# Layer 0's residual, first 1024 columns: transposed by VectorE in 32x32 blocks and placed by transfers, not by TensorE

## The chip, the cores and the metric

One core of one Trainium2 chip runs the whole program; the other cores are idle. The metric is device microseconds of one execution, as a median over runs. Engines are named as the profile names them: PE is TensorE's matmul side and PEld its weight loads, DVE is VectorE, ACT is ScalarE, POOL is GpSimd, and SP is the engine whose queue issues nearly all transfers. A transfer is issued by an engine's queue (SPq is SP's) and then moved by 16 DMA engines that all transfers share.

## The reference

A decoder trunk of two layers over 256 tokens of width 2048, all in float32. Layer 0 mixes the tokens with a gated MLP and a cross-attention, layer 1 with a latent attention (MLA) and a cross-attention; both end with a gated feed-forward block (width 5632) with a short causal convolution. Around the change this is what is computed (RMS norms written as `rmsnorm`):

```python
x = x + conv_ffn(rmsnorm(x, g_ffn[0]), w_ffn_up[0], conv_w[0], conv_b[0], w_ffn_down[0])   # end of layer 0
kv = rmsnorm(x, g_kv) @ w_kv_a            # start of layer 1: 2048 -> 512 + 64
c_kv = rmsnorm(kv[..., :512], g_kv_lat)
z = rmsnorm(x, g_mix[1]) @ w_in_b[0]
```

The products are made nearly float32-exact: each operand is split into a rounded high part and the rest (a low part), and three products (high by high, high by low, low by high) are added.

## The kernel before

**Layouts.** Outside the last part of the feed-forward block the residual stands feature-major, in the tile `xT` (`k.x`, 128 partitions by 16 blocks by 256 tokens): a partition is a feature, and a block is 128 features. Its two parts stand in `xhl` (two tiles of 8 blocks, each block 256 high and 256 low values), which is what every product reads. The feed-forward's down projection works the other way, token-major, on the tile `xt` (128 partitions by 2 token halves by 2048 features), so the residual is turned once before it (`Tokens.turn`, L1361 to L1368) and once after it, which is where the change lies.

**Turning to tokens (unchanged).** `turn(r)` lets DVE transpose 32x32 blocks of `xT` into a scratch tile `xs` (L1364), and four transfers on SP's queue place those blocks in `xt`, in pieces of 32 values, that is 128 bytes (L1368). It is done in four steps between the products of the up projection, for each of the two layers.

**The down projection.** Its rows come in three parts (`FF_GROUPS`), and each part has two phases `ph` of 1024 output columns. The stage of interest is the second phase of the last part in layer 0. It runs over six pairs of weight rows, n = 0 to 5. For each pair two weight tiles of 512 KB are loaded by SP's queue (L814, four buffers `raw` and two `gate`), split by ACT (high part, L709) and DVE (low part, L710), and used by 24 matmuls of 512 columns (L795, L796, L797). When a phase ends, DVE adds the sums to `xt` (`added`, L1407) and ACT takes squares for the next norm (L1430). Some of the first phase's work goes by a cheaper scheme whose sums go through `staged`, a tile in `xT`'s place, and are added to `xt` by `combine` (L1391 to L1398).

**Turning back.** The first phase of the last part completes columns 0 to 1023 of `xt`, the second phase columns 1024 to 2047. So the first half is turned back during the second phase: `Inner.begin` (L1422) hangs `turned(0)`, `turned(2)`, `turned(4)` and `turned(6)` behind the pairs n = 1 to 4 of that phase, each for two blocks. `turned` (L1432) lets PE transpose the four 128x128 squares of two blocks into one bank (`token_transpose`, L401, the matmuls are on L406), and `put` writes the high part (ACT, L1441), the low part (DVE, L1442) and the value itself into `xT` (ACT, L1443). The second half is turned in the same way behind the first products of layer 1 (`done`, L1447, `k.pending`); that isn't changed.

**What follows.** `layer_b` (L1079) begins with the product with `w_kv_a`: eight chunks of two blocks each, in the order of the blocks. Each chunk's weights (512 KB) are loaded by SP's queue (L108), split with a gain by ACT (L123) and DVE (L124) and used by 24 matmuls of 256 columns (L157, L158, L160). Chunk 0 needs blocks 0 and 1 of `xhl`, chunk 1 blocks 2 and 3, and so on.

**Order.** Each engine works through its own list in order. The lists are made before the run by a planner, which walks the program with a simulated clock and takes on each engine the instruction that stands earliest in the program among those it holds ready. The splits of the down projection are kept in their order by hand (`behind`, L700), and DVE's transposes and `combine` are kept in program order (`keep_in_program_order`). A transfer waits in SP's queue for its data and its buffer, and what stands behind it waits too.

Of the kernel before, what the change touches and what calls it, by code (L numbers as in the profile page):

```python
# [8 lines left out]
F32 = mybir.dt.float32  # L9
# [3 lines left out]
AF = mybir.ActivationFunctionType  # L13
ALU = mybir.AluOpType
AX = mybir.AxisListType

P = 128
D = 2048
S = 256
NB = D // P  # L20
# [1319 lines left out]
class Tokens:  # L1340
# [37 lines left out]
    def begin(self, ph, last):  # L1378
        self.ph, self.last = ph, last
        if ph == 0:  # L1380
            self.staged = self.k.ap.tile([P, 2, 4, 512], F32, tag="xT", name=self.k.uid("staged"))
        return {}
# [38 lines left out]
class Inner(Tokens):  # L1421
    def begin(self, ph, last):  # L1422
        super().begin(ph, last)
        return {"hooks": {n: [lambda n=n: self.turned(2 * n - 2)] for n in range(1, 5)}} if last and ph else {}

    def evict(self, tb, half, acc):
        j, o = self.added(tb, half, acc)
# [3 lines left out]

    def turned(self, k0):  # L1432
        k, nc = self.k, self.nc
        if k0 == 0:
            k.new_hl()
            k.x = k.ap.tile([P, NB, S], F32, tag="xT", name=k.uid("xT"))

        def put(b, acc):
            a = acc.rearrange("p (k s) -> p k s", k=2)
            hl = k.hl_tiles[b // 8][:, b % 8 : b % 8 + 2, :]  # L1440
            nc.scalar.activation(hl[:, :, :S], a, AF.Copy)  # L1441
            nc.vector.tensor_tensor(hl[:, :, S:], a, hl[:, :, :S].bitcast(F32), ALU.subtract)  # L1442
            nc.scalar.activation(k.x[:, b : b + 2, :], a, AF.Copy)  # L1443

        k.token_transpose(self.xt, k0, k0 + 2, put)
# [111 lines left out]
```

## Time and profile before

| | us |
|---|---|
| median of 3 runs | 2030.46 |
| lowest and highest run | 2029.62, 2032.41 |
| span of the profiled execution (first to last instruction) | 2027.8 |
| PE busy in that span | 2017.2 |
| DVE, ACT, POOL busy | 1618.2, 1167.1, 112.8 |

The profile gives for its execution the span alone, not a time of its own as the runs have it; the runs lie 1.8 to 4.6 us above the span, which is what lies around the first and the last instruction. Times inside the span are counted from its start. A matmul's row shows how long it was under way, and matmuls overlap, so a row's mean is not what it adds to the path; the chain of waits shows that, with the start of each piece and what it added.

### The profile page before, as it was taken

How to read it: one execution, taken by the hardware profiler on the slowest of the kernel's cores; microseconds unless marked ns; L12 is line 12 of the kernel's file. 1: busy time of each engine (PE TensorE's matmuls, PEld its weight loads, DVE VectorE, ACT ScalarE, POOL GpSimd, SP SyncE). 2: the span in 40 equal slices, each digit the busy share in tenths (PEclk: the TensorE clock that was granted, in tenths of full speed). 3: DMA queues.
4: the chain of work that ended last, by engine and by line, in shares of the span. 5: the costliest groups of instructions: out<-in, count | busy, mean ns of one | idle time of the engine just before them, and what ended most of it. 6: DMA issues, size and time to landing. Idle time of an engine off the chain costs nothing.

```text
span 2027.8 us, 38053 instructions
## 1 busy us (share of the span) xinstructions
PE 2017.2 (99%) x15136; PEld 1912.3 (94%) x15136; DVE 1618.2 (80%) x2433; ACT 1167.1 (58%) x1675; POOL 112.8 (6%) x169
## 2 busy tenths in 40 slices
PE   9999999999999999999999999999999999999998
PEld 8989999999889999899989999999988999889996
DVE  6866766778898788987878786777889878898787
ACT  6754744545565555655566675455566555565565
POOL 0000013100000000000002141400000000000000
PEclk9999999999999999999999999999999999999999
DMA  8876556688657676577656634568865767657764
GB/s 255 234 216 181 166 193 195 192 209 259 208 177 218 198 240 199 179 216 246 187 179 187 183 113 162 190 196 210 257 205 181 219 192 246 196 177 219 241 206 145
DMA packets 248263, 409.24 MB, mean 202 GB/s; under 512 B 71502, under 2 KB 78996, under 8 KB 248084
## 3 DMA queue, kind: packets, MB, share of 16 engines
q1 hardware_dynamic: 247892, 406.27, 65.4%
q8 instruction: 118, 1.93, 0.4%
q14 instruction: 61, 0.50, 0.1%
q10 hardware_dynamic: 192, 0.54, 0.1%
HBM read 400.46 MB, written 2.10 MB: 199 GB/s over the span
## 4 chain that ended last, share of the span: by engine, by line
PE 99%; DVE 0%; ACT 0%; issue 0%; ACTq 0%
PE ps L157 22%; PE ps L158 22%; PE ps L160 22%; PE ps L796 7%; PE ps L797 7%; PE ps L795 7%; PE ps L189 2%; PE ps L190 2%; PE ps L191 2%; PE ps L524 1%; PE ps L406 0%; PE ps L604 0%; PE ps L602 0%; PE ps L603 0%; PE ps L1236 0%; PE ps L1024 0%
## 5 line engine op out<-in xcount | busy, mean ns | idle before, releaser
L118 ACT ACTIVATE whi<-raw 128x1024 fp32r<-128x1024 f32 x484 | 512.7, 1061 | 513.1 <-PE ps L158 373.6
L119 DVE TENSOR_TENSOR wlo<-raw,whi 128x1024 fp32r<-128x1024 f32 x484 | 599.0, 1241 | 246.6 <-ACT whi L118 244.1
L157 PE MATMUL ps<-xhl,whi 128*128 128x256 f32 x3264 | 763.1, 277 | 0.0
L158 PE MATMUL ps<-xhl,whi 128*128 128x256 f32 x3264 | 761.5, 276 | 0.0
L158 PEld LDWEIGHTS ps<-xhl,whi 128*128 128x128 f32 x3264 | 612.8, 188 | 0.5
L157 PEld LDWEIGHTS ps<-xhl,whi 128*128 128x128 f32 x3264 | 612.7, 188 | 0.6
L160 PE MATMUL ps<-xhl,wlo 128*128 128x256 f32 x3264 | 436.6, 276 | 0.0
L160 PEld LDWEIGHTS ps<-xhl,wlo 128*128 128x128 f32 x3264 | 400.5, 188 | 0.0
L710 DVE TENSOR_TENSOR wlo<-raw,whi 128x1024 fp32r<-128x1024 f32 x112 | 134.3, 1220 | 31.5 <-ACT whi L709 30.3
L796 PE MATMUL ps<-wlo,h 128*128 128x512 f32 x404 | 157.3, 390 | 0.0
L797 PE MATMUL ps<-whi,h 128*128 128x512 f32 x404 | 157.2, 389 | 0.0
L709 ACT ACTIVATE whi<-raw 128x1024 fp32r<-128x1024 f32 x112 | 115.7, 1055 | 53.1 <-PE ps L158 37.3
L795 PE MATMUL ps<-whi,h 128*128 128x512 f32 x404 | 128.8, 390 | 0.0
L157 PE MATMUL ps<-mainhl,whi 128*128 128x256 f32 x512 | 119.7, 277 | 0.0
L158 PE MATMUL ps<-mainhl,whi 128*128 128x256 f32 x512 | 119.3, 276 | 0.0
L890 ACT ACTIVATE c<-a,cT 128x256 f32<-128x256 f32 x176 | 99.7, 592 | 32.2 <-DVE a L237 30.2
L709 ACT ACTIVATE whi<-xs 128x1024 fp32r<-128x1024 f32 x52 | 53.8, 1059 | 87.3 <-DVE xs L757 73.1
L158 PEld LDWEIGHTS ps<-mainhl,whi 128*128 128x128 f32 x512 | 96.0, 188 | 0.0
L157 PEld LDWEIGHTS ps<-mainhl,whi 128*128 128x128 f32 x512 | 95.9, 188 | 0.0
L795 PEld LDWEIGHTS ps<-whi,h 128*128 128x128 f32 x404 | 75.8, 188 | 15.7
L797 PEld LDWEIGHTS ps<-whi,h 128*128 128x128 f32 x404 | 75.8, 188 | 15.7
L796 PEld LDWEIGHTS ps<-wlo,h 128*128 128x128 f32 x404 | 75.9, 188 | 15.4
(378 smaller groups left out, 2896.6 us busy)
## 6 DMA issues: line engine op xcount, KB each, us to landing
raw<-in_w_ffn_up SPq DMA_DIRECT2D x352, 512.0 KB, 4.4
raw<-in_w_ffn_down SPq DMA_DIRECT2D x126, 512.0 KB, 4.5
raw<-in_w_out SPq DMA_DIRECT2D x64, 512.0 KB, 3.9
raw<-in_w_in_a SPq DMA_DIRECT2D x56, 512.0 KB, 4.2
gate<-in_w_ffn_down SPq DMA_DIRECT2D x38, 512.0 KB, 4.6
raw<-in_w_mem_kv SPq DMA_DIRECT2D x31, 512.0 KB, 4.8
sums<-in_w_ffn_down SPq DMA_DIRECT2D x48, 256.0 KB, 7.1
raw<-in_w_in_b SPq DMA_DIRECT2D x16, 512.0 KB, 4.1
```

The source lines that it names most:

```text
L118: nc.scalar.activation(hi[:, :n], raw[:, :n], AF.Copy)
L119: nc.vector.tensor_tensor(lo[:, :n], raw[:, :n], hi[:, :n].bitcast(F32), ALU.subtract)
L157: mm(acc[:, :S], wh, x[:, :S], start=first, stop=False)
L158: mm(acc[:, :S], wh, x[:, S:], start=False, stop=False)
L160: mm(acc[:, :S], wl, x[:, :S], start=False, stop=last)
L189: mm(acc, xh, wh, start=first, stop=False)
L709: self.behind(self.nc.scalar.activation(hi, w, AF.Copy))
L710: self.behind(self.nc.vector.tensor_tensor(lo, w, hi.bitcast(F32), ALU.subtract))
L795: mm(o, xh, wh, start=start, stop=False)
L796: mm(o, xh, wl, start=False, stop=False)
L797: mm(o, xl, wh, start=False, stop=stop)
L890: nc.scalar.activation(c, a, AF.Identity, scale=w(2), bias=w(3))
```

## The change

Columns 0 to 1023 of `xt` are no longer transposed by PE. After n = 1 and n = 2 of the last phase, `blocks(0)` and `blocks(1)` each take 512 columns (four blocks): DVE transposes 32x32 blocks into a scratch tile `xs`, once for each half of the tokens, and 16 transfers on SP's queue place them in `xT`, each 32 partitions by 8 pieces of 128 bytes. After n = 4 and n = 5, `operand` reads `xT` and writes the two parts of two blocks with one ACT and one DVE instruction; it is called for blocks 0 and 2 after n = 4, and for blocks 4 and 6 after n = 5. The tiles for `xhl` and `xT` are now taken in `blocks(0)`. Columns 1024 to 2047 are turned as before.

```diff
 class Inner(Tokens):
     def begin(self, ph, last):
         super().begin(ph, last)
-        return {"hooks": {n: [lambda n=n: self.turned(2 * n - 2)] for n in range(1, 5)}} if last and ph else {}
+        if not (last and ph):
+            return {}
+        hooks = {1 + h: [lambda h=h: self.blocks(h)] for h in range(2)}
+        hooks.update({n: [lambda b=b: self.operand(b) for b in range(4 * (n - 4), 4 * (n - 3), 2)] for n in (4, 5)})
+        return {"hooks": hooks}
+
+    def blocks(self, h):
+        k, nc = self.k, self.nc
+        if h == 0:
+            k.new_hl()
+            k.x = k.ap.tile([P, NB, S], F32, tag="xT", name=k.uid("xT"))
+        xs = k.tmp(self.pool, [P, 1024], "xs", 2)
+        s = xs.rearrange("p (r k a j) -> p r k a j", r=4, k=4, a=2)
+        for a in range(2):
+            src = self.xt[:, a, 512 * h : 512 * (h + 1)].rearrange("p (k r j) -> p r k j", r=4, j=32)
+            k.tc.keep_in_program_order(nc.vector.transpose(out=s[:, :, :, a], in_=src))
+        for r in range(4):
+            o = k.x[32 * r : 32 * (r + 1), 4 * h : 4 * (h + 1)].rearrange("i k (a q j) -> i q (k a) j", a=2, j=32)
+            for q in range(4):
+                nc.sync.dma_start(out=o[:, q], in_=s[32 * q : 32 * (q + 1), r].rearrange("i k a j -> i (k a) j"))
+
+    def operand(self, b):
+        k, nc = self.k, self.nc
+        x, hl = k.x[:, b : b + 2, :], k.hl_tiles[b // 8][:, b % 8 : b % 8 + 2, :]
+        nc.scalar.activation(hl[:, :, :S], x, AF.Copy)
+        nc.vector.tensor_tensor(hl[:, :, S:], x, hl[:, :, :S].bitcast(F32), ALU.subtract)
...
     def turned(self, k0):
         k, nc = self.k, self.nc
-        if k0 == 0:
-            k.new_hl()
-            k.x = k.ap.tile([P, NB, S], F32, tag="xT", name=k.uid("xT"))
```

## Rows read from the trace of the kernel before

**Rows 1.** The page: busy time by engine, and the clock granted to PE by slice.

```profile
PE 2017.2 (99%) x15136; PEld 1912.3 (94%) x15136; DVE 1618.2 (80%) x2433; ACT 1167.1 (58%) x1675; POOL 112.8 (6%) x169
...
PEclk9999999999999999999999999999999999999999
```

**Rows 2.** The page's chain that ended last, its shares by engine.

```profile
PE 99%; DVE 0%; ACT 0%; issue 0%; ACTq 0%
```

**Rows 3.** Busy time by 10 us stretch: each engine, clock, DMA share, GB/s.

```profile
1040.00:1050.00 10.00, 10.00 (x51) 8.30 (x50) 6.66 (x8) 7.16 (x14) 0.00 (x0) 1.00 0.66 205
1050.00:1060.00 10.00, 10.00 (x48) 8.24 (x47) 7.26 (x10) 6.14 (x12) 0.00 (x0) 1.00 0.24 79
```

**Rows 4.** The chain in order of time: start us, us added, piece.

```profile
1037.72 0.11 PE ps L406
...
1041.51 0.33 PE ps L406 x3
...
1043.70 0.44 PE ps L406 x4
...
1049.61 0.44 PE ps L406 x4
...
1055.54 0.43 PE ps L406 x4
...
1061.44 0.12 PE ps L157
...
1066.90 0.87 PE ps L406 x8
```

**Rows 5.** The transposes on L406 by source line: ns shortest/median/longest.

```profile
L406 PE MATMUL ps<-ident,xt x16: 270/272/273, 1037.6 to 1055.7; 128*128 128x128 f32 x16
```

**Rows 6.** Groups from 1037 to 1062: busy us, mean ns.

```profile
L1442 DVE TENSOR_TENSOR xhl<-ps,xhl 128x512 fp32r<-128x512 f32 x4 | 2.7, 685 | 1.1 <-ACT xhl L1441 1.1
...
L1443 ACT ACTIVATE xT<-ps 128x512 f32<-128x512 f32 x4 | 2.4, 594 | 3.2 <-DVE xhl L1442 3.2
L1441 ACT ACTIVATE xhl<-ps 128x512 fp32r<-128x512 f32 x4 | 2.3, 579 | 0.0
```

**Rows 7.** DVE in order of time: start us, us.

```profile
1038.32 1.22 DVE L1391 TENSOR_TENSOR xt<-xt,staged 128x1024 f32<-128x1024 f32 x1
...
1040.59 1.28 DVE L1407 TENSOR_TENSOR xt<-ps,xt 128x512 f32<-128x512 f32 x2
1041.79 1.21 DVE L710 TENSOR_TENSOR wlo<-raw,whi 128x1024 fp32r<-128x1024 f32 x1
```

**Rows 8.** DVE's block transposes on L1364 (1024 columns each), by source line.

```profile
L1364 DVE STREAM_TRANSPOSE xs<-xT x8: 1235/1240/1245, 412.5 to 1388.6; 128x1024 f32<-128x1024 f32 x8
...
  DMA xt<-xs: 1.5, 2
```

**Rows 9.** SP's issues by source line, ns: weights, then two kinds of 128-byte pieces.

```profile
L108 SPq DMA_DIRECT2D raw<-in_w_kv_a x8: 367/368/379, 1040.7 to 1065.0; - x8
...
L399 SPq DMA_DIRECT2D xraw<-in_x x32: 560/625/1169, 26.7 to 61.6; - x32
...
DMA to landing us min/median/max: 3.7/3.9/5.3
...
L1368 SPq DMA_DIRECT2D xt<-xs x32: 591/667/3811, 413.9 to 1398.8; - x32
```

**Rows 10.** SP in order of time, loads of w_kv_a: start us, us.

```profile
1043.03 0.38 SPq L108 DMA_DIRECT2D raw<-in_w_kv_a  x1
...
1046.32 1.50 SPq L108 DMA_DIRECT2D raw<-in_w_kv_a  x2
...
1057.15 0.37 SPq L108 DMA_DIRECT2D raw<-in_w_kv_a  x1
```

**Rows 11.** ACT in order of time: splits for n = 5 and for w_kv_a's chunks.

```profile
1048.96 2.01 ACT L709 ACTIVATE whi<-gate 128x1024 fp32r<-128x1024 f32 x2 [0.30 <-PE ps L797]
...
1054.95 2.56 ACT L123 ACTIVATE whi<-raw,gT 128x512 fp32r<-128x512 f32 x4 [1.30 <-PE ps L797]
```

## Prediction, as it was made before the result

> **What bounds the kernel now.** I read the page first, then the chain, then the stretch of the change. PE is busy for 2017.2 of 2027.8 us at the full clock in every slice [rows 1], which is the higher of its two levels (2.4 GHz), and 99% of the chain that ended last is PE [rows 2]. In the stretch of the change, 1037 to 1062 us, PE is busy without a gap, DVE for 6.7 to 7.3 us in ten and ACT for 6.1 to 7.2 [rows 3]. So nothing that ACT, DVE or SP save is worth any time here, and what they add costs none until it makes PE wait. The change can win only what its matmuls take on PE's path, and lose by making PE's operands late.
>
> **What is removed from PE.** Sixteen transposes, 0.27 us each under way [rows 5]. What they add to the path is in the chain: one for 0.11, three for 0.33, and three groups of four for 0.44, 0.44 and 0.43 [rows 4], together 1.75 us, or 0.11 each. The sixteen of the second half, unchanged, show the same price (0.87 for eight, [rows 4]). Gain: 1.75 us.
>
> A page of the Trainium skill speaks of another price: TensorE: Matmul & The Clock Gate, Part 4 (PE-mode transpose), gives about 275 ns for a transpose of 128x128 inside one kernel. By it the sum would be 16 x 0.275 = 4.4 us. The duration agrees with this trace (272), but the chain's step doesn't, as the transposes overlap.
>
> **What goes from ACT and DVE.** ACT loses the four copies into xT (4 x 0.594 us), keeps four high parts and DVE four low parts (579 and 685 ns, [rows 6]), now read from xT instead of PSUM. Worth nothing: neither engine is on the chain. DVE gains four block transposes of 512 columns. One of 1024 takes 1.24 us [rows 8], so about 0.65 each, 2.6 us in all. They need the finished columns, which are there after the last sum on L1407 at 1041.8 us (the last step of combine ends at 1039.5, [rows 7]). Ahead of the split that begins at 1041.79 they push it to 1045.5 at worst. That split is for n = 3, whose matmuls begin where the transposes of 1043.70 end (1044.14, [rows 4]); the second of its two weight tiles is wanted by about 1044.6, so it costs between 0 and 0.9 us. I take 0, because the first of the four can run before 1040.6 and a planner that puts the split first costs nothing.
>
> **What is added to SP and the transfers.** 32 issues, 16 for each half, each of 256 pieces of 128 bytes. No row has this size. Below is the weight load, also 256 pieces but long ones: 0.37 us each; above are the transfers with 128-byte pieces, 512 of them in 0.56 to 0.63 and 1024 in 0.59 to 0.67 [rows 9]. Between these I take 0.5 from start to start (nearest by count is the lower, by form the upper; ends 0.43 and 0.65 with the gap between issues). For landing I take 3.9 us, the median of the 64-KB transfers in 128-byte pieces [rows 9]. The movers have room: they are 24 to 66% busy between 1040 and 1060 [rows 3].
> - First half: its two transposes are done by about 1042.4. Sixteen issues at 0.5 make 8.0, with the three loads of w_kv_a that stand in this time [rows 10], 0.4 each, 9.2: the last is issued by 1051.6 and lands by 1055.5.
> - Second half: its issues follow, 8.0 more, last at 1059.6, landed by 1063.5. At 0.43 the landings are at 1054.4 and 1061.3, at 0.65 at 1057.9 and 1068.3.
>
> Behind the 32 in SP's queue stands the fifth load of w_kv_a (1057.15, [rows 10]). It would go at 1059.6, at worst 1064.4. It feeds chunk 4. The first chunk begins at 1061.44 on the chain and the transposes behind the second at 1066.90 [rows 4], so a chunk takes 2.73 us; behind chunks 1 and 2 come eight transposes each (0.87), so chunk 4 begins at 1074.1, or 1072.4 without the 1.75. A load issued at 1064.4 has some 4 us to land and, behind that, two splits on ACT of 0.64 (four take 2.56, [rows 11]) and a low part on DVE that I count at 0.7: it is there by 1070.4, 2 us early at worst. Cost 0.
>
> **What becomes a new wait.** `operand` waits on ACT for transfers, where the high part used to wait for PE. Blocks 0 and 1 are wanted by chunk 0 at 1061.4 less 1.75 = 1059.7. They are ready at 1055.5 + 0.58 + 0.69 = 1056.8 (1059.2 at the slow end): covered. Blocks 4 and 5 are wanted by chunk 2, behind the transposes of 1066.90, at 1066.90 + 0.87 - 1.75 = 1066.0. They are ready at 1063.5 + 1.27 = 1064.8: covered by 1.2 us, but not at the slow end (1069.6, 3.6 late). Queued behind a waiting `operand` on ACT are the splits of n = 5 (two at 1048.96) and of w_kv_a's chunks (four from 1054.95, [rows 11]), on DVE their low parts, and PE waits for all of these. This is the cover that the whole sum hangs on.
>
> **Sum.** -1.75 for PE, 0 for the rest: the span goes from 2027.8 to 2026.1. The page gives no time of its own for that execution; with the runs' median, 2.66 us above the span, the change gives 2030.46 - 1.75 = **2028.7 us**, 0.09% less. A measurement of this kernel tells about 0.2%, 4.1 us, from no change, so this counts as the same.
>
> **Rivals.**
> - *A late second half (B).* SP's issues go at 0.65 us, blocks 4 to 7 come 3.6 us late and PE waits once, at chunk 2: -1.75 + 3.6 = +1.9, 2032.3 us; from 2029.5 to 2034.5 over its bounds. For: the rows for 128-byte pieces all lie at 0.56 and above, and one of the issues took 3.8 us [rows 9]. Against: a quarter to a half of the pieces per issue. Still the same within 0.2%.
> - *ACT's list in the wrong order (C), slower.* If the planner believes the transfers to land earlier than they do, it places `operand` ahead of splits that PE needs sooner. ACT then stands at blocks 4 and 5 until 1068.3 with chunk 1's split behind it: two `operand` steps, two splits and a low part make it 1068.3 + 1.2 + 1.3 + 0.7 = 1071.5 where PE wants it at 1062.4 (1059.7 + 2.73): 9.1 - 1.75 = +7.4, 2038 us. The same with the first half, ahead of n = 5's splits, gives 6 us of stall, as these are wanted at 1055.97 - 1.75 = 1054.2 and the first comes at 1057.9 + 1.2 + 1.1 = 1060.2; that stall would be part of the other, not added to it. It decides against the change from a stall of 5.8 us (4.1 + 1.75). For: the planner's clock was behind the transfers where it last handled 128-byte pieces between engines (DVE waited 1.5 us on two transfers into xt, [rows 8]). Against: that was only 1.5 us in two places, and n = 5's splits end at 1051.0, 5 us ahead of PE [rows 11].
> - *The transposes cost more than their steps (D), faster.* If each took its 272 ns from the path [rows 5], the gain would be 4.35 us and the time 2026.1, 0.21% less. Against it stands the chain: four take 0.44 us and the next matmul starts right behind them [rows 4]. The page named above would give this.
>
> **How the numbers follow.** Forecast (A: covered, 2027.7 to 2029.7 with the spread of the runs) 0.46; B 0.24; C 0.26; D 0.04. A and B are within 0.2%: same 0.70, slower 0.26, faster 0.04. The range leaves out D and the worse half of C: 2027.5 to 2037.5. Below, A's gain is bounded by the 1.75 us; above, it holds B's bounds and C with a single late operand.
>
> **What would show it.** Right: the 16 transposes gone between 1037 and 1056 in the chain, no PE wait before `w_kv_a`'s chunks, and the pairs of n some 5.5 us apart instead of 5.9 (1049.61 to 1055.54, [rows 4]). SP's 32 issues in one row at about 0.5 us, first half landed before 1056 and second before 1065. B: PE idle ahead of chunk 2, ended by the low or high part of xhl. C: ACT idle on a transfer into xT ahead of a weight split, and PE idle behind that split. Wrong altogether: a time below 2026, or a PE that waits for a weight load that SP issued late, which I hold covered.

## The result and the profile after

The change takes 2034.3 us against 2030.42 for the kernel before (medians of 21 runs each): a ratio of 1.0021, with a 95% interval of 1.0015 to 1.0027. That is 3.9 us slower, where 1.75 us faster was forecast. One of the change's 21 runs took 2531.7 us at a mean granted clock of 0.75 and isn't in the ratio. The interval is 1.2 us to either side, so this loss, of a size that the prediction counted as the same, is told from no change. The time lies inside the stated range, but on the wrong side of the kernel before, and between the rival of a late second half and the rival of ACT's list. The profiled execution has a span of 2031.7 us (2027.8 before), so it carries the same 3.9 us.

First the page of the changed kernel, the line that answers to [rows 1] and the one that answers to [rows 2]:

```profile
PE 2017.4 (99%) x15120; PEld 1912.3 (94%) x15120; DVE 1620.0 (80%) x2437; ACT 1165.0 (57%) x1671; POOL 113.1 (6%) x169
...
PE 96%; DVE 1%; SPq 1%; ACT 1%; issue 1%; DMA 0%; ACTq 0%; DVEq 0%
```

PE has its 16 instructions less. The chain, which was 99% PE, now leaves PE for SP's queue, a transfer and ACT. Where, PE in order of time shows (start us, us, piece, and the idle time before it with what ended it):

```profile
1059.48 0.28 PE L157 MATMUL ps<-xhl,whi 128*128 128x256 f32 x1
...
1062.22 1.91 PE L406 MATMUL ps<-ident,xt 128*128 128x128 f32 x16
1067.37 0.70 PE L270 MATMUL ps<-ssum,ones 128*128 128x256 f32 x2 [3.24 <-ACT xT L1465]
1068.95 0.58 PE L157 MATMUL ps<-xhl,whi 128*128 128x256 f32 x1 [0.88 <-ACT whi L123]
...
1073.22 0.28 PE L157 MATMUL ps<-xhl,whi 128*128 128x256 f32 x1
```

Up to 1059.48 the forecast holds: chunk 0 of `w_kv_a` begins there, where the same matmul began at 1061.28 before, 1.80 us earlier. This execution was already 0.16 us later ahead of the stretch, as one ACT instruction shows (before, then the change), so that the start moved by 1.96 us:

```profile
999.95 1.33 ACT L890 ACTIVATE c<-a,cT 128x256 f32<-128x256 f32 x2 [2.56 <-DVE a L237]
```

```profile
1000.11 1.33 ACT L890 ACTIVATE c<-a,cT 128x256 f32<-128x256 f32 x2 [2.56 <-DVE a L237]
```

Behind chunk 0 PE's list has the 16 transposes of the second half, then two matmuls of a norm (L270), which wait 3.24 us for ACT's copies on L1465, then chunk 1, which waits another 0.88 us for the split of its weights: 4.1 us in all. Chunk 1 is also slow: chunk 2 begins 4.3 us later, where a chunk took 2.73 [rows 4]. The busy time by stretch has the reason (after the engines: granted clock, DMA share, GB/s):

```profile
1050.00:1060.00 10.00, 10.00 (x48) 8.37 (x47) 5.75 (x9) 3.67 (x8) 0.00 (x0) 1.00 0.32 51
...
1066.00:1068.00 2.00, 0.63 (x2) 0.30 (x2) 1.81 (x3) 2.00 (x5) 2.00 (x7) 1.00 1.04 396
1068.00:1070.00 2.00, 1.12 (x6) 1.05 (x6) 1.49 (x3) 2.00 (x4) 0.57 (x3) 0.64 1.06 407
1070.00:1072.00 2.00, 2.00 (x11) 2.00 (x11) 1.67 (x3) 1.98 (x4) 0.00 (x0) 0.50 0.80 231
1072.00:1074.00 2.00, 2.00 (x19) 2.00 (x19) 1.00 (x1) 1.99 (x4) 0.00 (x0) 1.00 0.89 275
```

After PE's two waits the granted clock falls to 0.50 (1.2 GHz, the lower level) and is back at 1.00 (2.4 GHz) by 1072: some 1.5 us for chunk 1. The sum is -1.8 + 4.1 + 1.5 = +3.8, against 3.9 in the span.

One thing that PE waited for begins on SP's queue. In order of time, and the new line by itself (ns shortest/median/longest, and the landings):

```profile
1041.42 0.38 SPq L108 DMA_DIRECT2D raw<-in_w_kv_a  x1
1042.04 21.73 SPq L1443 DMA_DIRECT2D xT<-xs  x32
1063.87 12.51 SPq L108 DMA_DIRECT2D raw<-in_w_kv_a  x7
```

```profile
L1443 SPq DMA_DIRECT2D xT<-xs x32: 585/609/1434, 1042.0 to 1063.2; - x32
...
DMA to landing us min/median/max: 1.9/2.0/2.8
```

The 32 issues take 21.7 us without a break. Only one load of `w_kv_a` stands ahead of them. The second, chunk 1's weights, was issued at 1043.03 before [rows 10] and is now issued at 1063.87, twenty microseconds later; the third and fourth follow it.

The chain in order of time tells another story for the same stretch (start us, us added, piece):

```profile
1063.16 1.96 DMA xT<-xs
1065.13 0.03 ACTq L1448
1065.15 0.04 issue
1065.20 1.15 ACT xhl L1448 x2
1066.35 0.48 ACT xhl L1463
1066.83 1.46 ACT xT L1465 x3
1068.29 0.62 ACT whi L123
```

Here the last of the small transfers lands at 1065.1, ACT makes the high parts of blocks 4 to 7 (L1448), which it had to wait for, then the copies behind it (L1465), which end PE's first wait, and only then splits chunk 1's weights (L123). Both stories end at this split. Which of them costs the time, the profile doesn't say: if chunk 1's weights, issued at 1063.87, take the 4.2 us that the same load takes in the second run below, they come at 1068.1 (an estimate), nearly the same moment as ACT gets to them.

### The profile page after: what moved, and what is told of

It is laid out like the page before. It is cut to its first block, busy times and chain, and to the rows that moved or that the text cites. A ratio compares the mean times of both kernels' runs of the same rounds, so it can differ in the third digit from the quotient of the medians.

```text
span 2031.7 us, 38064 instructions
## 1 busy us (share of the span) xinstructions
PE 2017.4 (99%) x15120; PEld 1912.3 (94%) x15120; DVE 1620.0 (80%) x2437; ACT 1165.0 (57%) x1671; POOL 113.1 (6%) x169
## 4 chain that ended last, share of the span: by engine, by line
PE 96%; DVE 1%; SPq 1%; ACT 1%; issue 1%; DMA 0%; ACTq 0%; DVEq 0%
PE ps L157 22%; PE ps L158 22%; PE ps L160 22%; PE ps L795 7%; PE ps L796 7%; PE ps L797 7%; PE ps L189 2%; PE ps L190 2%; PE ps L191 2%; PE ps L524 1%; SPq L1443 1%; PE ps L604 0%; PE ps L602 0%; PE ps L603 0%; PE ps L1236 0%
```

## The experiments

Three theories. **Queue:** the weights of chunks 1 to 3 stand behind the 32 issues on SP. **Operand:** ACT stands at blocks 4 to 7 and holds what PE needs. **Clock:** PE's lower clock behind the wait is the larger part. The first four runs share 33 runs of the kernel before, with a median of 2029.64; the last three share 27, with 2030.45.

**Loads on another queue.** The first four loads of `w_kv_a` go out on ACT's queue; the 32 issues stay on SP.

```diff
 # chunk()
-        self.last_raw = nc.sync.dma_start(out=view(raw), in_=src).ins.name
+        queue = nc.sync
+        if getattr(self, "early", 0):
+            queue, self.early = nc.scalar, self.early - 1
+        self.last_raw = queue.dma_start(out=view(raw), in_=src).ins.name
 # layer_b(), ahead of the product with w_kv_a
+            self.early = 4
```

> The change, with the first four loads of w_kv_a issued from ACT's queue instead of SP's, so that they no longer stand behind the 32 issues. Three theories of the 3.9 us lost. Queue (the weights of chunks 1 to 3 are issued only after the 32 issues): the time falls to 2029 to 2030 us, as only chunk 2 can still wait some 0.5 us for blocks 4 to 7, and chunk 1's splits are done before 1062. Operand (ACT stands at blocks 4 to 7 until their transfers land, with the work that PE needs behind it): ACT still waits until about 1065, the time stays at 2032.5 or above. Clock (PE's lower clock behind a wait is the larger part): follows whichever wait is left; without one, the granted clock stays at 1.00.

Measured: 2028.2 us, ratio 0.9993 (0.9984 to 1.0001). SP, and the one wait that PE has left between 1030 and 1090 us (waiter, what it waited for, us, times, longest; line numbers are three or four higher in this kernel):

```profile
1041.74 23.37 SPq L1447 DMA_DIRECT2D xT<-xs  x32
1065.21 2.08 SPq L111 DMA_DIRECT2D raw<-in_w_kv_a  x4
```

```profile
PE ps L160 <- ACT xhl L1452: 0.8, 1, 0.8
```

The 32 issues take 23.4 us, 1.6 more than in the change, and ACT still waits for the second half (until 1066.8). But PE loses only 0.8 us, at chunk 2, and the granted clock stays at 1.00. With the loads in time the whole loss is gone; the kernel is 1.4 us below before by the medians, but the interval holds no change. That is what Queue expected; Operand expected 2032.5 or more. The loads of chunks 4 to 7, behind the 32 at 1065.2 here, cost nothing.

The run moves more than the loads, though. ACT's list has another order (the splits of chunks 0 and 1, the split of chunk 3, then `operand` for blocks 4 to 7):

```profile
1053.38 2.56 ACT L126 ACTIVATE whi<-raw,gT 128x512 fp32r<-128x512 f32 x4 [2.62 <-PE ps L800]
...
1060.73 1.32 ACT L126 ACTIVATE whi<-raw,gT 128x512 fp32r<-128x512 f32 x2
...
1066.77 1.15 ACT L1452 ACTIVATE xhl<-xT 128x512 fp32r<-128x512 f32 x2 [3.35 <-DMA xT<-xs]
```

In the change chunk 1's split stood behind that `operand`; with the loads early the planner puts it ahead. So this run shows that without the late loads there is no loss. What ACT's wait would cost in the change's own order, with the loads in time, neither this run nor another shows.

**ACT spared the wait.** SP's order is left as it is, and the high parts of blocks 4 to 7 are made on DVE.

```diff
 # operand()
-        nc.scalar.activation(hl[:, :, :S], x, AF.Copy)
+        if b < 4:
+            nc.scalar.activation(hl[:, :, :S], x, AF.Copy)
+        else:
+            nc.vector.tensor_copy(hl[:, :, :S], x)
```

> The change, with the high part of blocks 4 to 7 made by DVE instead of ACT, so that ACT waits for no transfer of the second half; SP's order is as in the change (one load of w_kv_a, then the 32 issues, then the rest). Queue: the weights of chunk 1 still land at about 1067.5, so the time stays at 2033 to 2035 us. Operand: PE's wait ahead of chunk 1 goes, 2029 to 2031 us.

Measured: 2033.52 us, ratio 1.002 (1.0011 to 1.0029), the same as the change. Its chain and PE's longest wait:

```profile
1062.70 0.45 ACT xhl L1466
1063.15 4.21 DMA raw<-in_w_kv_a
1067.39 0.73 ACT whi L123
```

```profile
PE ps L157 <- ACT whi L123: 2.2, 1, 2.2
PE ps L270 <- ACT xT L1468: 1.3, 1, 1.3
```

With ACT's wait gone (DVE waits 0.5 us for these blocks instead) the chain goes straight through the late weight load (issued at 1063.15, 4.2 us to land) to the same split, 0.9 us earlier than in the change. PE waits 3.5 us in all, 0.6 less than in the change, but its lower clock lasts longer: chunk 1 takes 5.3 us from its start to chunk 2's, where it took 4.3.

```profile
1068.16 0.58 PE L157 MATMUL ps<-xhl,whi 128*128 128x256 f32 x1 [2.15 <-ACT whi L123]
...
1073.45 0.29 PE L157 MATMUL ps<-xhl,whi 128*128 128x256 f32 x1
```

So the late loads are enough for the loss by themselves, and the chain of the changed kernel named the one of two nearly equal waits whose removal alone gains nothing.

**Only the first 512 columns.** The second 512 go by PE as before.

```diff
-        hooks = {1 + h: [lambda h=h: self.blocks(h)] for h in range(2)}
-        hooks.update({n: [lambda b=b: self.operand(b) for b in range(4 * (n - 4), 4 * (n - 3), 2)] for n in (4, 5)})
+        hooks = {1: [lambda: self.blocks(0)], 4: [lambda: self.operand(0), lambda: self.operand(2)]}
+        hooks.update({n: hooks.get(n, []) + [lambda n=n: self.turned(2 * n - 2)] for n in (3, 4)})
```

> Only the first 512 columns go by DVE and transfers (16 issues), the second 512 by PE as before. Queue: SP is done with the 16 at about 1053 and the loads of chunks 1 to 3 follow in time, so half the gain is left and no wait: 2030.4 - 0.9 = 2029.5 us, at most 2030.2. Operand: the first half's transfers land at 1054.7 in the change, five us before chunk 0, so the same 2029.5. Over 2031.5 both are wrong, and the moved order of PE's list or the first half's wait on ACT costs more than I hold.

Measured: 2028.71 us, 0.93 below before by the medians, ratio 0.9994 (0.9985 to 1.0003). SP is free at 1052.8, and PE waits for nothing from 1030 to 1090:

```profile
1041.51 11.27 SPq L1443 DMA_DIRECT2D xT<-xs  x16
1052.88 13.75 SPq L108 DMA_DIRECT2D raw<-in_w_kv_a  x7
```

Half of the change by itself costs no wait; the interval holds no change too, so the half gain isn't shown.

**The issues alone.** The kernel before, all its PE transposes kept, with the DVE transposes and the 32 issues added to it; their target is scratch in the second half of `xhl`.

```diff
 # Inner.begin(): beside turned(0) to turned(6)
+        for h in range(2):
+            hooks[1 + h].append(lambda h=h: self.blocks(h))
 # blocks(), as in the change but for the target
+        scratch = k.hl_tiles[1][:, 2 * h : 2 * h + 2, :].bitcast(F32).rearrange("p k s -> p (k s)").rearrange("p (k s) -> p k s", k=4)
...
+            o = scratch[32 * r : 32 * (r + 1)].rearrange("i k (a q j) -> i q (k a) j", a=2, j=32)
+            for q in range(4):
+                nc.sync.dma_start(out=o[:, q], in_=s[32 * q : 32 * (q + 1), r].rearrange("i k a j -> i (k a) j"))
```

> The kernel before, with all of its transposes on PE, and the change's four DVE transposes and 32 issues added to it; they write scratch that nothing reads. Here two loads of w_kv_a stand ahead of the 32 issues in SP's list, so that the third is the first to be late. Queue: it is issued at about 1064 where chunk 2 is wanted at 1067.8, so PE waits 1.5 to 3 us there, and with a lower clock behind it the time is 2031.5 to 2034.5 us. Operand: no instruction that PE needs waits for the transfers, 2030 to 2030.9 us.

Measured: 2035.94 us, ratio 1.0026 (1.0017 to 1.0035), that is 5.3 us (3.5 to 7.1) above before. SP, then PE's idle times, then two steps of the chain:

```profile
1045.64 20.90 SPq L1442 DMA_DIRECT2D xhl<-xs  x32
1066.64 9.46 SPq L108 DMA_DIRECT2D raw<-in_w_kv_a  x6
```

```profile
1070.27 0.70 PE L270 MATMUL ps<-ssum,ones 128*128 128x256 f32 x2 [1.92 <-ACT xT L1461]
1071.55 0.58 PE L157 MATMUL ps<-xhl,whi 128*128 128x256 f32 x1 [0.58 <-ACT whi L123]
```

```profile
1066.64 4.12 DMA raw<-in_w_kv_a
...
1070.78 0.73 ACT whi L123
```

No product reads what is moved here, and yet the kernel loses more than the change does. The chain goes from the issues through chunk 2's late load to its split. The loss is more than I expected (the median lies 1.4 us above my upper end). PE's waits aren't the reason: they are 2.5 us, where I had 1.5 to 3. What I had too low is the clock. Chunk 2 takes 5.3 us from 1071.55, and the chunk behind it 3.2, where a chunk took 2.73, some 3.0 us more together:

```profile
1076.84 0.42 PE L157 MATMUL ps<-xhl,whi 128*128 128x256 f32 x1
...
1080.00 0.28 PE L157 MATMUL ps<-xhl,whi 128*128 128x256 f32 x1
```

Waits and clock make 5.5 us, against 5.3 by the ratio. (This profiled execution, the longest of its runs at 2038.4, has a further PE wait of 1.8 us far away, between 1410 and 1415 us.) The run isn't quite free of ACT's wait: ACT stood 0.5 us for the moved blocks, as a high part of the second half (L1459) is written over the scratch. With the transposes' 1.96 us taken off, 5.3 - 1.96 = 3.3, near the change's 3.9, but the interval is too wide to read PE's gain from it.

**Half as many issues.** All 1024 columns in one step, with two DVE transposes of 1024 columns into blocks 8 to 15 of `xT`, which are unused until later, and 16 issues of 512 pieces.

```diff
-        hooks = {1 + h: [lambda h=h: self.blocks(h)] for h in range(2)}
+        hooks = {1: [self.blocks]}
 # blocks()
-        xs = k.tmp(self.pool, [P, 1024], "xs", 2)
-        s = xs.rearrange("p (r k a j) -> p r k a j", r=4, k=4, a=2)
+        xs = k.x[:, 8:].rearrange("p k s -> p (k s)")
+        s = xs.rearrange("p (r k a j) -> p r k a j", r=4, k=8, a=2)
...
-            o = k.x[32 * r : 32 * (r + 1), 4 * h : 4 * (h + 1)].rearrange("i k (a q j) -> i q (k a) j", a=2, j=32)
+            o = k.x[32 * r : 32 * (r + 1), :8].rearrange("i k (a q j) -> i q (k a) j", a=2, j=32)
```

> All 1024 columns in one step: two DVE transposes of 1024 columns into blocks 8 to 15 of xT, which are still unused, and 16 issues of 512 pieces in place of 32 of 256. Two loads of w_kv_a stand ahead of the 16. If an issue costs its 0.61 us whatever number of pieces it has, SP is done about 1057 to 1058, the third load follows in time and there is no wait for weights; the data lands at about 1059, so chunk 0 may wait 0.5 to 1.5 us for blocks 0 and 1: 0.2 to 1.3 us below the kernel before. If SP's time goes with the pieces, the 16 take 21 us as the 32 did, chunk 0 waits for its data until 1068, and the time is 5 us or more above the kernel before.

Measured: 2027.96 us, ratio 0.9989 (0.9980 to 0.9998), the only version whose interval lies below the kernel before. Its line by itself and SP in order of time (this execution was already 2 us later than the change's ahead of this stretch):

```profile
L1442 SPq DMA_DIRECT2D xT<-xT x16: 591/627/1578, 1047.3 to 1058.3; - x16
```

```profile
1042.71 2.71 SPq L108 DMA_DIRECT2D raw<-in_w_kv_a  x2
1047.32 11.63 SPq L1442 DMA_DIRECT2D xT<-xT  x16
1059.05 9.15 SPq L108 DMA_DIRECT2D raw<-in_w_kv_a  x6
```

Twice the pieces cost 0.627 us an issue instead of 0.609: SP's time goes by the issue, not by the piece. PE waits for nothing from 1030 to 1090 us, and chunk 0 didn't wait for its blocks as I had allowed for, so the gain is larger than the 0.2 to 1.3 expected: 2.2 us by the ratio, 0.4 to 4.1 by its interval, which holds the 1.75.

**The second half on POOL's queue.**

```diff
-                nc.sync.dma_start(out=o[:, q], in_=s[32 * q : 32 * (q + 1), r].rearrange("i k a j -> i (k a) j"))
+                (nc.gpsimd if h else nc.sync).dma_start(out=o[:, q], in_=s[32 * q : 32 * (q + 1), r].rearrange("i k a j -> i (k a) j"))
```

> The change, with the second half's 16 issues on POOL's queue, so that SP has only 16 and the loads of chunks 1 to 3 follow them at about 1052. Queue: no wait for weights. What POOL takes for an issue no row shows: up to 1.1 us each, the second half lands before chunk 2 wants it and the time is 1.2 to 1.8 us below the kernel before; at 2 us each it lands at about 1080 and the time is 10 us above. Operand (ACT's wait for the second half alone): the time goes with that landing in the same way, so this run tells only the price of POOL's queue.

Measured: 2033.56 us, ratio 1.0015 (1.0006 to 1.0023), neither of the two outcomes I had. POOL's issues were cheap and done early; ACT was late by its own list:

```profile
L1443 POOL DMA_DIRECT2D xT<-xs x16: 582/582/747, 1048.9 to 1057.7; - x16
```

```profile
1067.31 1.32 ACT L123 ACTIVATE whi<-raw,gT 128x512 fp32r<-128x512 f32 x2
1068.54 1.53 ACT L1463 ACTIVATE xhl<-ps 128x512 fp32r<-128x512 f32 x3
1069.97 1.15 ACT L1448 ACTIVATE xhl<-xT 128x512 fp32r<-128x512 f32 x2
```

```profile
1070.65 0.94 PE L157 MATMUL ps<-xhl,whi 128*128 128x256 f32 x4 [2.12 <-ACT xhl L1448]
```

ACT reaches blocks 4 to 7 (L1448) without a wait for a transfer, behind six chunks' splits, two of which waited for loads (0.7 us together), and three high parts of the second half. PE waits 2.1 us for it. So this run doesn't tell what POOL's queue is worth; it shows that the planner's order on ACT can also cost time by placing `operand` too late, where the rival feared it too early.

**Three loads on ACT.** As the first run, but chunk 0's load stays on SP.

```diff
-            queue, self.early = nc.scalar, self.early - 1
+            queue, self.early = (nc.sync if self.early == 4 else nc.scalar), self.early - 1
```

> As the run with four loads on ACT's queue, but chunk 0's load stays on SP, where it stands ahead of the 32 issues in any case: three loads (chunks 1 to 3) on ACT. Queue: the same 1.2 to 1.7 us below the kernel before, ratio 0.9992 to 0.9994, as only these three were late in the change. If the ratio is above 0.9998, the gain of the first such run was chance.

Measured: 2028.81 us, 1.6 below before by the medians, ratio 0.9995 (0.9986 to 1.0004). PE's one wait is 1.2 us, at chunk 2. The estimate is a ten-thousandth above what I expected and the interval holds that too. It holds no change as well, so for the loads on ACT what the two runs show is that the loss goes; that they beat the kernel before is likely but not shown.

## Why the prediction was wrong, step by step

- **PE's gain: right, a little low.** Chunk 0 begins 1.96 us earlier, counted from the same ACT instruction in both traces, against 1.75 by the chain's steps; the five other versions without these sixteen transposes show 1.96 or 1.97 too. That the transposes cost their 272 ns each (4.4 us by the Trainium skill's page, TensorE: Matmul & The Clock Gate, Part 4) is excluded by the same start.
- **DVE's block transposes: right.** Four of 0.70 us, 2.8 us under way, and no PE wait for a split of n = 3.
- **The price of an issue: taken too low.** I took 0.5 us between 0.43 and 0.65, start to start. It is 0.609 for the issue and 0.65 from start to start, the upper end: 21.7 us for 32, where 16 were summed. The row nearest in form (128-byte pieces, 0.56 to 0.67, [rows 9]) was right, not the one nearest in count.
- **The landing: taken too high.** 2.0 us, not 3.9. The two errors partly cancel: the second half landed at 1065.1, against 1063.5.
- **The step that failed** is in SP's sum: "with the three loads of w_kv_a that stand in this time", and then "Behind the 32 in SP's queue stands the fifth load". I kept the times that the loads of chunks 1 to 3 had in the trace before, as if they had a claim on them. They stand later in the program than `blocks`, and the planner, which goes by that, put all 32 issues ahead of three of the four. So the load that had to be covered was chunk 1's, wanted at 1062.4, and not chunk 4's, wanted at 1072.4. Issued at 1063.87, it couldn't be. I had named the queue and what stands behind it, and counted from the wrong load. It is the last of the prediction's own signs of being wrong altogether, "a PE that waits for a weight load that SP issued late, which I hold covered". Late loads are enough for the loss (the runs with ACT spared and with the issues alone), and with them on another queue it is gone (ratios 0.9993 and 0.9995).
- **The rivals.** ACT's wait came, as B and C had it: 4.8 us at the first half, with nothing behind it that PE needed by then, and 0.8 us at the second half. There the order that C feared came true: the copies that end PE's first wait (L1465) and chunk 1's split stood behind it on ACT. But it was short, as the second half landed at 1065.1 and not at 1068.3, and the run without it gains nothing, because the same thing had happened on SP's list: work that PE needs behind work that takes long. Once the loads were in time, B's wait at chunk 2 cost PE 0.8 and 1.2 us, under its price of 3.6.
- **The clock** was in no step: PE at its lower clock after its waits costs some 1.5 us in the change beside 4.1 us of waits, so it isn't the larger part there. It is 2.6 beside 3.5 where ACT is spared, and 3.0 beside 2.5 with the issues alone. That is read from the starts of the chunks and was not tried by itself. In the two runs with loads on ACT the clock stayed at 1.00.

## What to carry to other kernels

When an edit adds issues to a queue, don't take the old order of that queue for granted: write down what stands later in the program, let all of it wait behind the new block, and check the first of those, not the one that the old trace would put there. Here many small transfers were paid on the queue that issued them, by the issue; fewer and larger issues took the loss away, and so did another queue for the loads that must not wait. Where two waits end at the same time, the chain names one: only taking each away by itself tells which one costs. And such a run is worth a look at every engine's list, since an edit on one queue can reorder another.

## What the runs showed of the hardware

An issue of 256 pieces of 128 bytes from SBUF to SBUF took 0.609 us on SP's queue, one of 512 pieces 0.627, and 256 pieces on POOL's queue 0.582, where a weight load of 512 KB took 0.37 [rows 9]. Each landed 2.0 us after its issue (median of the change's 32), while SP issued one behind the other; so in a series SP was the limit and not the movers, which were 32% busy from 1050 to 1060 us.

The Trainium skill's page DMA: Bandwidth & Descriptors, section Issuing engines are not separate DMA queues, says that the time to initiate a transfer is usually small beside the transfer itself. In this trace it isn't: 0.61 of 2.0 us, and 21.7 us for the series, behind which the loads came late.

I had not expected the clock to fall here: after PE's 3.2 and 0.9 us of waiting between 1064 and 1069 us the granted clock was 0.50 in the stretch from 1070 to 1072 us, and 1.00 again in the next, with PE busy in both.
